# Half of the second MLP product as seven half-size products, with the sums folded into the residual

## The chip, the core and the metric

The kernel runs on one NeuronCore of one Trainium2 chip. The metric is the device time of one execution in microseconds. Three runs of the kernel before gave 973.18, 973.82 and 974.45 us; the median is 973.82 us.

Engine names are those of the profile: PE multiplies matrices (PEld loads its stationary operand), DVE does elementwise work on two tensors, ACT does elementwise work on one tensor and converts types, POOL and SP here mostly issue DMA transfers. Each engine executes its own list of instructions.

## The reference, cut to what matters

One layer of a decoder trunk on 512 tokens of width 1024, in float32. Only the MLP block is touched:

```python
D_MODEL = 1024; SEQ = 512; D_FF = 4 * D_MODEL
h2 = rmsnorm(x, ln2)
x = x + jnp.square(jax.nn.relu(h2 @ w_mlp1)) @ w_mlp2        # (512 x 1024) @ (1024 x 4096), then (512 x 4096) @ (4096 x 1024)
h3 = rmsnorm(x, ln3)
x = x + jax.nn.sigmoid(h3 @ w_pg) * (p @ w_pp)
return rmsnorm(x, ln_f)
```

## The kernel before, in words

**Layout.** Activations lie feature-major: a tile `u` holds 128 features in the partitions and the 512 tokens in the free dimension. The residual is `xx[0..7]`, eight such tiles. The hidden layer of the MLP is `hid[0..31]`, 32 tiles. All `u` tiles come from one pool of `NU` = 71 buffers.

**Precision.** Every product is made in three: each operand is split into a high and a low part of the format that PE reads, and `three` issues high x high, high x low, low x high into one accumulator. A split is one ACT instruction for the high part (`split_hi`, L347 or L349; L236 for weights) and one DVE instruction for the low part (`split_lo`, L355 or L357; L231 for weights).

**Weights.** The host cuts the weights into units of 128 x 1024 numbers (`weight_units`, `_layout`). `OPERANDS` is the order in which PE uses them. When the program asks for operand i with `weight`, `fetch` first emits, for later operands: the low part of operand i+2 (DVE), the high part of i+3 (ACT), sums of weights for i+4, and the load of i+5 (SP). So weights are prepared two operands ahead, in the order of the program. There are four buffers for low parts, five for high parts, six for raw units.

**A plain product** over two 128-feature tiles of input (one "tm" unit, `m2s{sub}.{kk}`) is 24 matmuls with 512 moving columns: 2 input tiles x 4 output tiles x 3. The second MLP product has two halves of its output (`sub` 0 and 1, four PSUM accumulators each) and 16 such units each: 2 x 16 x 24 = 768 matmuls of 512 columns.

**Seven products for eight.** `strassen` multiplies a 2 x 2 block matrix by seven products of half-size blocks instead of eight. Stage i of the seven multiplies one weight operand (A11, S1, A22, S2, A12, S4, S3) by one activation operand (B11, T1, T4, T2, B21, B22, T3) with 24 matmuls of 256 moving columns. S and T are sums or differences of blocks. The S of the weights are made by two DVE additions (L210, L216) and two DMA transfers that add as they write (L202, L213, issued by POOL). The seven products go to four PSUM banks a, c, d, b, with bank a used in stages 0, 3 and 6, c in 1 and 5, d in 2, b in 4. `BEGIN` and `END` say when a bank is read: after stages 0, 1, 2 and 3 the bank is copied to a `u` tile on ACT (`begin`, L322); after stages 4, 5, 6 and 6 the bank is added to such a tile on DVE (`end`, which calls `finish` and `add`, L340). A later stage that writes into the same bank has to wait for the read before it. The first MLP product is eight such groups of seven (`quad`).

**PSUM.** There are two pools of four banks: `mmt` and `smt`. `strassen` takes `mmt`. In the second MLP product `sub` 0 takes its four accumulators from `mmt`, `sub` 1 from `smt`.

**The order around the change** is written by the program itself. `run` issues matmuls in pieces of eight; after each piece `step` takes one item off the list `later`, and, if enough columns have passed (`pace`, 2048 as a rule, which eight matmuls of 256 columns are), advances the generator at the head of the list `side` by one `yield`. So a stage of seven-product work has three steps, and one unit of plain work has three. `drain` steps until both lists are empty without issuing matmuls. The items' instructions go to the engines in the order in which they are emitted.

**After an output half** is complete, four times: `t = psum * norm2` (L1244), `xx += t` (L1245), then `normed` puts on `later` a first item (L349 on ACT: high part; L380 on ACT: square) and, from that, a second item (L357 on DVE: low part; L1111 on DVE: sum of squares).

Of the kernel before, what the change touches and what calls it, by code (L numbers as in the profile page):

```python
# [13 lines left out]
AF = mybir.ActivationFunctionType  # L14
OP = mybir.AluOpType
# [25 lines left out]

def weight_units():
# [13 lines left out]
    def quad(name, src, col, kind="quad"):  # L56
        for m, k in ((0, 0), (1, 0), (1, 1), (0, 1)):
            u.append((f"{name}.A{m + 1}{k + 1}", kind, src, k, col + m * (P if kind == "quad" else 256)))
# [25 lines left out]
    for sub in range(2):  # L84
        for kk in range(16):
            u.append((f"m2s{sub}.{kk}", "tm", "w_mlp2", kk * 2 * P, sub * 512))
# [55 lines left out]
def block_kernel(ctx, tc, xT, ws, pT, wts, wha, wa2, vec, lnf, rel, onehot, ident_d, mask_d, out):  # L142
# [150 lines left out]
    def strassen(name, xo, finish, tm=False, scale=1.0, extra=None):  # L293
# [3 lines left out]
        bank, sums = {}, {}  # L297
# [21 lines left out]
        def begin(c, b):  # L319
            def go():  # L320
                sums[c] = u32()
                S.activation(sums[c], bank[b], AF.Copy, scale=-scale if c[0] else scale)  # L322
            later.insert(0, go)
# [852 lines left out]
    hid = [None] * 32  # L1176
# [4 lines left out]
    def quad(q):  # L1181


        def finish(m, t, s, ps):
            add(m, s, s, ps)

            def positive():
                V.tensor_scalar(s, s, 0.0, None, op0=OP.max)  # L1188

            def act():  # L1190
                for n in range(2):
                    j = 4 * q + 2 * n + m
                    if hid[j] is None:
                        hid[j] = u32()
                    S.activation(hid[j][:, halves(t)], s[:, halves(n)], AF.Square)  # L1195

            later.extend([positive, act])

        def extra(i):
            if i in (3, 4):  # L1200
                later.append(lambda: hid_split(i - 3))

        strassen(f"m1q{q}", x1_op, finish, extra=extra if q == 7 else None)

    hs = {}

    def hid_split(k):
        if k < 32:
            hs[k] = split(hid[k])

    for q in range(8):
        quad(q)
    for k in (2, 3):
        hid_split(k)
# [3 lines left out]
    for sub in range(2):  # L1218
        pss = [mmt() if sub == 0 else smt() for _ in range(4)]
        for kk in range(16):  # L1220
            wh, wl = weight(f"m2s{sub}.{kk}")
            mms = []
            for k in (2 * kk, 2 * kk + 1):
                xh, xl = hs.pop(k)
                for o in range(4):
                    c = slice((k % 2) * 512 + o * P, (k % 2) * 512 + (o + 1) * P)
                    mms += [(pss[o], wh[:, c], xh, k == 0, False), (pss[o], wh[:, c], xl, False, False),
                            (pss[o], wl[:, c], xh, False, k == 31)]
            run(mms)
            for k in (2 * kk + 4, 2 * kk + 5):  # L1230
                hid_split(k if k < 32 or sub else k - 32)
            if sub == 1 and kk == 8:
                for k in range(2):
                    t = u32()
                    GP.dma_start(t, pT[k * P:(k + 1) * P, :])
                    pt.append(split(t))
                for g in range(2):
                    t = u32()
                    GP.dma_start(t, lnf[:, g * 512:(g + 1) * 512].to_broadcast([P, 512]))
                    lnb.append(t)  # L1240
        for o in range(4):
            j = 4 * sub + o
            t = u32()
            V.tensor_tensor(t, pss[o], norm2[1], op=OP.mult)  # L1244
            V.tensor_tensor(xx[j], xx[j], t, op=OP.add)  # L1245
            normed(j, C_LN3, x2s, acc2)
# [126 lines left out]
def _layout(inputs):  # L1373
# [3 lines left out]
    for i, (_, kind, s, r, c) in enumerate(UNITS):  # L1377
# [8 lines left out]
        elif kind == "quad":  # L1386

            a = w.reshape(4, 2, P, -1)[:, r, :, c:c + 3 * P]
# [44 lines left out]
```

## Time and profile before

| what | number |
|---|---|
| median of three runs | 973.82 us |
| the profiled execution, its own time | 974.23 us |
| its span from first to last instruction | 972.4 us |
| granted PE clock, mean | 0.998 |
| first MLP product ends, second begins (on PE) | 730.72 us |
| `sub` 0 ends, `sub` 1 begins | 817.95 us |
| `sub` 1 ends | 904.99 us |

Times inside the span count from its first instruction. In a row of a timeline the columns are: start, length (of the whole group, if it says x2 or more), engine, line, operation, what it writes and reads, and in brackets how long the engine stood idle before it and what it then waited for. The length of an instruction is longer than its distance to the next one on the same engine where the two overlap; both are read below.

### The profile page before, as it was taken

How to read it: one execution, taken by the hardware profiler on the slowest of the kernel's cores; microseconds unless marked ns; L12 is line 12 of the kernel's file. 1: busy time of each engine (PE TensorE's matmuls, PEld its weight loads, DVE VectorE, ACT ScalarE, POOL GpSimd, SP SyncE). 2: the span in 40 equal slices, each digit the busy share in tenths (PEclk: the TensorE clock that was granted, in tenths of full speed). 3: DMA queues.
4: the chain of work that ended last, by engine and by line, in shares of the span. 5: the costliest groups of instructions: out<-in, count | busy, mean ns of one | idle time of the engine just before them, and what ended most of it. 6: DMA issues, size and time to landing. Idle time of an engine off the chain costs nothing.

```text
span 972.4 us, 16047 instructions
## 1 busy us (share of the span) xinstructions
PE 963.5 (99%) x6444; PEld 885.8 (91%) x6444; DVE 694.8 (71%) x988; ACT 524.9 (54%) x878; POOL 96.6 (10%) x137
## 2 busy tenths in 40 slices
PE   9999999999999999999999999999999999999997
PEld 7789999999998999999988889999998888888886
DVE  7788879676788769977855798777676446653654
ACT  7347546345657667575822456556565335442633
POOL 0140010420001021022010000101000000000000
PEclk9999999999999999999999999999999999999999
DMA  8465554974446555546645437566543332533102
GB/s 296 161 197 126 148 139 123 242 205 119 110 120 185 151 131 131 131 131 195 170 112 193 111 64 197 135 169 158 168 132 129 98 98 69 169 91 104 44 1 86
DMA packets 40314, 134.67 MB, mean 138 GB/s; under 512 B 5235, under 2 KB 6847, under 8 KB 40240
## 3 DMA queue, kind: packets, MB, share of 16 engines
q1 hardware_dynamic: 27936, 93.29, 29.1%
q0 software_dynamic: 11008, 38.01, 19.5%
q10 hardware_dynamic: 1296, 2.36, 0.6%
q8 instruction: 50, 0.82, 0.3%
q14 instruction: 24, 0.20, 0.1%
HBM read 127.31 MB, written 8.17 MB: 139 GB/s over the span
## 4 chain that ended last, share of the span: by engine, by line
PE 96%; DVE 2%; issue 1%; DMA 1%; ACT 0%; SPq 0%; POOLq 0%; POOL 0%; DVEq 0%
PE mmt L250 78%; PE smt L250 10%; PE smt L853 1%; PE smt L793 1%; PE smt L719 1%; PE mmt L468 1%; DMA u<-in_xT_dram 1%; PE mmt L469 0%; DVE lo L231 0%; PE mmt L467 0%; DVE ur L355 0%; PE smt L810 0%; PE smt L690 0%; PE smt L809 0%; PE smt L799 0%
## 5 line engine op out<-in xcount | busy, mean ns | idle before, releaser
L250 PE MATMUL mmt<-ur,hi 128*128 128x256 f32 (+1 forms) x2832 | 605.7, 310 | 0.0
L250 PEld LDWEIGHTS mmt<-ur,hi 128*128 128x128 f32 x2832 | 460.4, 188 | 30.0 <-issue 1.9
L250 PE MATMUL mmt<-ur,lo 128*128 128x256 f32 (+1 forms) x1416 | 438.5, 310 | 0.8 <-DVE lo L231 0.8
L231 DVE TENSOR_TENSOR lo<-w,hi 128x1024 fp32r<-128x1024 f32 x239 | 290.1, 1220 | 108.5 <-PE mmt L250 63.6
L236 ACT ACTIVATE hi<-w 128x1024 fp32r<-128x1024 f32 x239 | 250.0, 1054 | 130.1 <-issue 73.1
L250 PEld LDWEIGHTS mmt<-ur,lo 128*128 128x128 f32 x1416 | 266.7, 188 | 15.6 <-DVE lo L231 1.2
L250 PE MATMUL mmt<-hi,ur 128*128 128x256 f32 (+3 forms) x736 | 155.5, 306 | 0.0
L347 ACT ACTIVATE ur<-u 128x512 fp32r<-128x512 f32 x136 | 80.1, 621 | 86.5 <-DVE u L1088 30.9
L250 PEld LDWEIGHTS mmt<-hi,ur 128*128 128x128 f32 x736 | 118.9, 189 | 5.5
L250 PE MATMUL mmt<-lo,ur 128*128 128x256 f32 (+3 forms) x368 | 112.3, 305 | 0.0
L355 DVE TENSOR_TENSOR ur<-u,ur 128x512 fp32r<-128x512 f32 x135 | 88.9, 687 | 17.0 <-ACT ur L347 16.4
L322 ACT ACTIVATE u<-mmt 128x512 f32<-128x512 f32 x96 | 57.0, 593 | 54.2 <-PE mmt L250 54.1
L340 DVE TENSOR_TENSOR u<-u,mmt 128x512 f32<-128x512 f32 (+1 forms) x100 | 62.2, 650 | 32.2 <-PE mmt L250 32.1
L250 PE MATMUL smt<-ur,hi 128*128 128x512 f32 x272 | 83.8, 389 | 0.0
L250 PEld LDWEIGHTS mmt<-lo,ur 128*128 128x128 f32 x368 | 69.4, 189 | 2.6
L250 PEld LDWEIGHTS smt<-ur,hi 128*128 128x128 f32 x272 | 51.1, 188 | 10.7
L250 PE MATMUL smt<-ur,lo 128*128 128x512 f32 x136 | 53.0, 390 | 0.0
L213 POOL DMA_DIRECT2D w<-in_wts_dram x24 | 21.4, 893 | 278.3 <-DVE w L210 166.3
L202 POOL DMA_DIRECT2D w<-in_wts_dram x24 | 21.6, 901 | 237.8 <-DVE lo L231 50.2
L1195 ACT ACTIVATE u<-u 128x256 f32<-128x256 f32 x64 | 23.0, 409 | 30.5 <-DVE u L1188 30.5
L250 PEld LDWEIGHTS smt<-ur,lo 128*128 128x128 f32 x136 | 25.5, 188 | 5.2
L216 DVE TENSOR_TENSOR w<-w 128x1024 f32<-128x1024 f32 x24 | 29.4, 1225 | 0.8
(206 smaller groups left out, 706.4 us busy)
## 6 DMA issues: line engine op xcount, KB each, us to landing
w<-in_wts_dram SPq DMA_DIRECT2D x167, 512.0 KB, 3.9
w<-in_wts_dram POOLq DMA_DIRECT2D x48, 512.0 KB, 5.6
u<-in_xT_dram SPq DMA_DIRECT2D x8, 256.0 KB, 4.9
v_dram<-u POOLq DMA_DIRECT2D x8, 256.0 KB, 7.1
u<-v_dram POOLq DMA_DIRECT2D x8, 256.0 KB, 7.0
y_dram<-u ACTq DMA_DIRECT2D x8, 256.0 KB, 2.3
u<-y_dram POOLq DMA_DIRECT2D x8, 256.0 KB, 7.0
u<-in_xT_dram POOLq DMA_DIRECT2D x8, 256.0 KB, 8.6
```

Source lines behind the costliest of these rows:

```text
L202: GP.dma_start(w, wts[UNIT[f"{q}.A22"]], accum_op=OP.add)
L213: GP.dma_start(w, wts[UNIT[f"{q}.A21"]], accum_op=OP.add)
L216: V.tensor_tensor(w, w, raw[f"{q}.A12"], op=OP.add)
L231: V.tensor_tensor(lo, w, hi.bitcast(F32), op=OP.subtract)
L236: S.activation(hi, w, AF.Copy)
L250: TE.matmul(o, lhsT=l, rhs=r, start=a, stop=b, skip_group_check=shared)
L322: S.activation(sums[c], bank[b], AF.Copy, scale=-scale if c[0] else scale)
L340: V.tensor_tensor(out, s, ps, op=OP.subtract if m else OP.add)
L347: S.activation(hi, x, AF.Copy)
L355: V.tensor_tensor(lo, x, hi.bitcast(F32), op=OP.subtract)
L468: TE.matmul(q0ps[i], lhsT=hi[:, c], rhs=xl, start=False, stop=False)
L1195: S.activation(hid[j][:, halves(t)], s[:, halves(n)], AF.Square)
```

## The change

The 32 hidden tiles are cut into four chunks of eight. Chunks 0 and 2 are multiplied as before ("plain"), chunks 1 and 3 by `strassen` ("seven"), each for both output halves. The order on PE, from the list `MLP2`, is: plain 0 for `sub` 0; seven 1 for `sub` 0; seven 1 for `sub` 1; plain 2 for `sub` 0; seven 3 for `sub` 0; seven 3 for `sub` 1; plain 0 for `sub` 1; plain 2 for `sub` 1. The accumulators of `sub` 0 now come from `smt`, those of `sub` 1 from `mmt`.

`hid_sums` makes the seven activation operands of a chunk, as side work, once for both output halves. The tiles of chunks 1 and 3 are squared in place and kept as blocks (`hb`). The four result tiles of a seven-product group are kept in `msum[sub]`; the second group of the same half is given them as `acc`, and then `begin` is an addition on DVE instead of a copy on ACT. When the last group of a half is done there is a `drain`, and `folds(sub)` is put on `side`: four times a multiplication by `norm2` and two additions of 256 columns into `xx`, and for `sub` 0 after these the four finals (L1244, L1245 and `normed` of before). For `sub` 1 the finals come after the last plain chunk, as before.

The plain chunks 0 and 2 are split once for each output half, as all chunks were. Four splits are put on `later` in the last four stages of the group in front of a plain chunk (`first_splits`). The two small loads for the next product (`pT`, `lnf`) are emitted after the first plain chunk of `sub` 1.

```diff
--- before.py
+++ after.py
@@ -39,6 +39,11 @@
 QUADS = ("quad", "quadt")
 
 
+MLP2 = (("plain", 0, 0), ("seven", 0, 1), ("seven", 1, 1), ("plain", 0, 2), ("seven", 0, 3), ("seven", 1, 3),
+        ("plain", 1, 0), ("plain", 1, 2))
+SEVEN = sorted({c for what, _, c in MLP2 if what == "seven"})
+
+
 def weight_units():
 
     u = []
@@ -53,9 +58,9 @@
 
     fm("q0", "w_in", att_col(0, 0), 4)
     u = u[NS:]
-    def quad(name, src, col, kind="quad"):
+    def quad(name, src, col, kind="quad", chunk=0):
         for m, k in ((0, 0), (1, 0), (1, 1), (0, 1)):
-            u.append((f"{name}.A{m + 1}{k + 1}", kind, src, k, col + m * (P if kind == "quad" else 256)))
+            u.append((f"{name}.A{m + 1}{k + 1}", kind, src, 2 * chunk + k, col + m * (P if kind == "quad" else 256)))
 
     fm("k0", "w_in", att_col(0, 1), 4)
     fm("q1", "w_in", att_col(1, 0), 4)
@@ -81,9 +86,12 @@
     fm("wo", "w_out", 0, 8)
     for q in range(8):
         quad(f"m1q{q}", "w_mlp1", q * 512)
-    for sub in range(2):
-        for kk in range(16):
-            u.append((f"m2s{sub}.{kk}", "tm", "w_mlp2", kk * 2 * P, sub * 512))
+    for what, sub, c in MLP2:
+        if what == "plain":
+            for kk in range(4 * c, 4 * c + 4):
+                u.append((f"m2s{sub}.{kk}", "tm", "w_mlp2", kk * 2 * P, sub * 512))
+        else:
+            quad(f"m2s{sub}c{c}", "w_mlp2", sub * 512, chunk=c)
     for j in range(2):
         u.append((f"pp{j}.0", "tm", "w_pp", 0, j * 512))
     for j in range(2):
@@ -290,11 +298,11 @@
     def halves(t):
         return slice(t * HT, (t + 1) * HT)
 
-    def strassen(name, xo, finish, tm=False, scale=1.0, extra=None):
-
-
-
-        bank, sums = {}, {}
+    def strassen(name, xo, finish, tm=False, scale=1.0, extra=None, acc=None):
+
+
+
+        bank, sums = {}, acc or {}
 
         def stage(op, xname, b):
             wh, wl = weight(f"{name}.{op}")
@@ -318,6 +326,8 @@
 
         def begin(c, b):
             def go():
+                if acc:
+                    return add(c[0], sums[c], sums[c], bank[b])
                 sums[c] = u32()
                 S.activation(sums[c], bank[b], AF.Copy, scale=-scale if c[0] else scale)
             later.insert(0, go)
@@ -1173,7 +1183,7 @@
     side.append(rms_gen(acc1, norm2, 30, 4, True))
 
 
-    hid = [None] * 32
+    hid, hb, hx = [None] * 32, {}, {}
 
     def x1_op(name, pr):
         return cols(xop[name, pr // 2], halves(pr % 2))
@@ -1188,6 +1198,10 @@
                 V.tensor_scalar(s, s, 0.0, None, op0=OP.max)
 
             def act():
+                if q // 2 in SEVEN:
+                    S.activation(s, s, AF.Square)
+                    hb[q, m, t] = s
+                    return
                 for n in range(2):
                     j = 4 * q + 2 * n + m
                     if hid[j] is None:
@@ -1196,54 +1210,147 @@
 
             later.extend([positive, act])
 
+        strassen(f"m1q{q}", x1_op, finish, extra=first_splits(0) if q == 7 else None)
+
+    hs = {}
+    plain = [8 * c + k for what, _, c in MLP2 if what == "plain" for k in range(8)]
+    ahead = [0]
+
+    def hid_splits(n):
+        for k in plain[ahead[0]:ahead[0] + n]:
+            hs[k] = split(hid[k])
+        ahead[0] += n
+
+    def first_splits(n):
+
         def extra(i):
-            if i in (3, 4):
-                later.append(lambda: hid_split(i - 3))
-
-        strassen(f"m1q{q}", x1_op, finish, extra=extra if q == 7 else None)
-
-    hs = {}
-
-    def hid_split(k):
-        if k < 32:
-            hs[k] = split(hid[k])
+            if 3 <= i:
+                later.append(lambda: hid_splits(1))
+        return extra
+
+    def hid_sums(c):
+
+        def blocks(k, t):
+            return [hb[2 * c + g, k, t] for g in range(2)]
+
+        def sums(f, *args):
+            res = [u32() for _ in range(2)]
+            for o, *x in zip(res, *args):
+                f(o, *x)
+            return res
+
+        def less(o, a, b):
+            V.tensor_tensor(o, a, b, op=OP.subtract)
+
+        def splits(name, ts):
+            his = [split_hi(t) for t in ts]
+            yield
+            for g in range(2):
+                hx[name, c, g] = split_lo(ts[g], his[g])
+            yield
+
+        b11, b12, b21, b22 = blocks(0, 0), blocks(0, 1), blocks(1, 0), blocks(1, 1)
+        yield from splits("B11", b11)
+        t1 = sums(less, b11, b12)
+        yield from splits("T1", t1)
+        t2 = sums(minus, t1, b22)
+        yield
+        t4 = sums(minus, t2, b21)
+        yield from splits("T4", t4)
+        yield from splits("T2", t2)
+        yield from splits("B21", b21)
+        yield from splits("B22", b22)
+        t3 = sums(less, b22, b12)
+        yield from splits("T3", t3)
 
     for q in range(8):
         quad(q)
-    for k in (2, 3):
-        hid_split(k)
     drain()
     x2s, acc2 = [None] * KC, []
     pt, lnb = [], []
-    for sub in range(2):
-        pss = [mmt() if sub == 0 else smt() for _ in range(4)]
-        for kk in range(16):
+    pss, msum = [None, None], [{}, {}]
+
+    def fold(sub, m, t):
+
+        x = msum[sub][m, t]
+        x3 = x.rearrange("p (n c) -> p n c", n=2)
+        V.tensor_tensor(x3, x3, norm2[1][:, None, halves(t)].to_broadcast([P, 2, HT]), op=OP.mult)
+        yield
+        for n in range(2):
+            o = xx[4 * sub + 2 * n + m][:, halves(t)]
+            V.tensor_tensor(o, o, x[:, halves(n)], op=OP.add)
+        yield
+
+    def finals(sub):
+
+        for o in range(4):
+            j = 4 * sub + o
+            t = u32()
+            V.tensor_tensor(t, pss[sub][o], norm2[1], op=OP.mult)
+            V.tensor_tensor(xx[j], xx[j], t, op=OP.add)
+            normed(j, C_LN3, x2s, acc2)
+            yield
+
+    def folds(sub):
+        for k in sorted(msum[sub]):
+            yield from fold(sub, *k)
+        yield from finals(sub) if not sub else ()
+
+    def m2_seven(sub, c, last):
+        def finish(m, t, x, ps):
+            add(m, x, x, ps)
+            msum[sub][m, t] = x
+
+        def xo(name, pr):
+            return cols(hx[name, c, pr // 2], halves(pr % 2))
+
+        strassen(f"m2s{sub}c{c}", xo, finish, extra=first_splits(0) if last else None,
+                 acc=msum[sub])
+
+    def m2_plain(sub, c, first, last):
+        if first:
+            pss[sub] = [mmt() if sub else smt() for _ in range(4)]
+        for kk in range(4 * c, 4 * c + 4):
             wh, wl = weight(f"m2s{sub}.{kk}")
             mms = []
             for k in (2 * kk, 2 * kk + 1):
                 xh, xl = hs.pop(k)
                 for o in range(4):
-                    c = slice((k % 2) * 512 + o * P, (k % 2) * 512 + (o + 1) * P)
-                    mms += [(pss[o], wh[:, c], xh, k == 0, False), (pss[o], wh[:, c], xl, False, False),
-                            (pss[o], wl[:, c], xh, False, k == 31)]
+                    w = slice((k % 2) * 512 + o * P, (k % 2) * 512 + (o + 1) * P)
+                    p, a, b = pss[sub][o], first and k == 8 * c, last and k == 8 * c + 7
+                    mms += [(p, wh[:, w], xh, a, False), (p, wh[:, w], xl, False, False), (p, wl[:, w], xh, False, b)]
             run(mms)
-            for k in (2 * kk + 4, 2 * kk + 5):
-                hid_split(k if k < 32 or sub else k - 32)
-            if sub == 1 and kk == 8:
-                for k in range(2):
-                    t = u32()
-                    GP.dma_start(t, pT[k * P:(k + 1) * P, :])
-                    pt.append(split(t))
-                for g in range(2):
-                    t = u32()
-                    GP.dma_start(t, lnf[:, g * 512:(g + 1) * 512].to_broadcast([P, 512]))
-                    lnb.append(t)
-        for o in range(4):
-            j = 4 * sub + o
-            t = u32()
-            V.tensor_tensor(t, pss[o], norm2[1], op=OP.mult)
-            V.tensor_tensor(xx[j], xx[j], t, op=OP.add)
-            normed(j, C_LN3, x2s, acc2)
+
+            if ahead[0] < len(plain) and (kk % 4 < 2 or step_[0] + 1 < len(MLP2) and MLP2[step_[0] + 1][0] == "plain"):
+                hid_splits(2)
+
+    side.append(hid_sums(1))
+    step_ = [0]
+    order = {sub: [i for i, (what, o, _) in enumerate(MLP2) if what == "plain" and o == sub] for sub in range(2)}
+    for i, (what, sub, c) in enumerate(MLP2):
+        step_[0] = i
+        if what == "seven":
+            if sub and c != SEVEN[-1]:
+                side.append(hid_sums(SEVEN[-1]))
+                pace[0] = 6144
+            m2_seven(sub, c, MLP2[i + 1][0] == "plain")
+            pace[0] = 2048
+            if c == SEVEN[-1]:
+                drain()
+                side.append(folds(sub))
+            continue
+        m2_plain(sub, c, i == order[sub][0], i == order[sub][-1])
+        if i == len(MLP2) - 2:
+            for k in range(2):
+                t = u32()
+                GP.dma_start(t, pT[k * P:(k + 1) * P, :])
+                pt.append(split(t))
+            for g in range(2):
+                t = u32()
+                GP.dma_start(t, lnf[:, g * 512:(g + 1) * 512].to_broadcast([P, 512]))
+                lnb.append(t)
+    for _ in finals(1):
+        pass
     while later:
         step()
 
@@ -1385,7 +1492,7 @@
             a = w.reshape(4, 2, P, -1)[:, r, :, c:c + 256].transpose(1, 0, 2)
         elif kind == "quad":
 
-            a = w.reshape(4, 2, P, -1)[:, r, :, c:c + 3 * P]
+            a = w[r // 2 * D:(r // 2 + 1) * D].reshape(4, 2, P, -1)[:, r % 2, :, c:c + 3 * P]
             a = np.stack([a[..., :P], a[..., 2 * P:]], axis=2).transpose(1, 0, 2, 3)
         else:
             a = w[:, c:c + 256].reshape(4, P, 2, P).transpose(1, 2, 0, 3)
```

## The prediction

> **What bounds the kernel now.** I read the page's busy times first, then the chain of work that ended last, then the stages by window. All three in this order:
>
> ```profile
> span 972.4 us, 16047 instructions
> PE 963.5 (99%) x6444; PEld 885.8 (91%) x6444; DVE 694.8 (71%) x988; ACT 524.9 (54%) x878; POOL 96.6 (10%) x137
> ...
> 610.31 207.64 PE mmt L250 x1400
> 817.95 87.04 PE smt L250 x384
> ...
> 581.27:730.72 149.45, 149.45 (x1256) 149.36 (x1257) 113.28 (x135) 91.39 (x149) 10.45 (x12) 1.00 0.61 162
> 730.72:817.95 87.23, 87.23 (x387) 72.24 (x386) 43.80 (x55) 36.26 (x54) 0.00 (x0) 1.00 0.31 98
> 817.95:904.99 87.04, 87.04 (x385) 72.07 (x385) 47.74 (x62) 36.20 (x54) 2.18 (x4) 1.00 0.35 109
> ```
>
> PE is busy 99%; from 610.31 to 904.99 us the chain is nothing but matmuls, at granted clock 1.00. The window rows give PE, PEld, DVE, ACT, POOL: in the seven-product stage (first row) DVE is at 113.28 of 149.45, 76%; in the two plain halves at 43.80 and 47.74 of 87, half idle. So whatever shortens PE's work shortens the kernel, as long as DVE's added work stays out of PE's way. Both have to be priced.
>
> **PE's gain.** The distance between equal events gives the price of a group without its modelled ends. DVE's rows of one seven-product group and of the plain units:
>
> ```profile
> 685.34 0.69 DVE L340 TENSOR_TENSOR u<-u,mmt 128x512 f32<-128x512 f32 x1 [1.57 <-PE mmt L250]
> 686.06 0.43 DVE L1188 TENSOR_SCALAR u<-u 128x512 f32<-128x512 f32 x1
> 686.41 1.22 DVE L231 TENSOR_TENSOR lo<-w,hi 128x1024 fp32r<-128x1024 f32 x1
> 687.66 1.23 DVE L210 TENSOR_TENSOR w<-w 128x1024 f32<-128x1024 f32 x1
> 688.80 0.68 DVE L340 TENSOR_TENSOR u<-u,mmt 128x512 f32<-128x512 f32 x1
> ...
> 691.04 1.29 DVE L340 TENSOR_TENSOR u<-u,mmt 128x512 f32<-128x512 f32 x2
> 692.24 0.42 DVE L1188 TENSOR_SCALAR u<-u 128x512 f32<-128x512 f32 x1
> ...
> 705.28 0.69 DVE L340 TENSOR_TENSOR u<-u,mmt 128x512 f32<-128x512 f32 x1 [1.56 <-PE mmt L250]
> ...
> 747.26 1.23 DVE L231 TENSOR_TENSOR lo<-w,hi 128x1024 fp32r<-128x1024 f32 x1 [2.71 <-PE mmt L250]
> 748.70 1.29 DVE L355 TENSOR_TENSOR ur<-u,ur 128x512 fp32r<-128x512 f32 x2 [0.21 <-ACT ur L347]
> ...
> 807.10 1.23 DVE L231 TENSOR_TENSOR lo<-w,hi 128x1024 fp32r<-128x1024 f32 x1 [2.71 <-PE mmt L250]
> ```
>
> 685.34 and 705.28 are the same addition of two neighbouring groups: 19.94 us for 168 matmuls of 256 columns, 0.1187 us each, 2.85 us a stage. 747.26 and 807.10 are eleven plain units apart: 59.84 / 11 = 5.44 us for 24 matmuls of 512 columns, 0.2267 us each. A chunk of four units costs 21.76 us plain and 19.94 us by seven, 1.82 us less; four times, **7.28 us less**. The arithmetic falls by an eighth, the time by 8.4%, because a short matmul costs more than half a long one.
>
> [...]
>
> **DVE's prices**, as distance to the next instruction, since neighbours overlap:
>
> ```profile
> 580.00 4.62 DVE L231 TENSOR_TENSOR lo<-w,hi 128x1024 fp32r<-128x1024 f32 x4
> ...
> 338.71 0.76 DVE L1045 TENSOR_TENSOR u<-u 128x256 f32<-128x256 f32 x2 [0.70 <-ACT u L1041]
> ...
> 815.94 0.69 DVE L1244 TENSOR_TENSOR u<-mmt,rstd 128x512 f32<-128x512 f32 x1 [6.11 <-PE mmt L250]
> 816.67 0.69 DVE L1245 TENSOR_TENSOR u<-u 128x512 f32<-128x512 f32 x1
> 817.28 0.68 DVE L1244 TENSOR_TENSOR u<-mmt,rstd 128x512 f32<-128x512 f32 x1
> ...
> 908.30 0.74 DVE L357 SCALAR_TENSOR_TENSOR ur<-u,cv,ur 128x512 fp32r<-128x512 f32 x1
> 908.96 0.68 DVE L1111 TENSOR_TENSOR u<-u 128x512 f32<-128x512 f32 x1
> 909.56 0.75 DVE L357 SCALAR_TENSOR_TENSOR ur<-u,cv,ur 128x512 fp32r<-128x512 f32 x1
> ```
>
> Low part of a weight: (4.62 - 1.22) / 3 = 1.13. Weight sum behind it: 688.80 - 687.66 = 1.14, and 0.11 for waiting on that low part (687.66 - 686.41 = 1.25). Any independent 512-column operation (L340 x2, L355 x2): 0.60. 256 columns: 0.76 - 0.42 = 0.34. Fold, not in the trace: its multiplication and dependent addition are priced like L1244 and L1245, 0.73, then two of 0.34: 1.41. Bounds for it: 0.60 + 0.68 below, 0.73 + 0.84 (lengths) above. A final: 0.73 + 0.61 = 1.34. The second item of `normed`: 0.66 + 0.60 = 1.26.
>
> **Where the cover holds.** I added up what each part of the new order puts on DVE, in the order of the lists: plain 0 / `sub` 0: 19.6 of 21.76 us (four low parts, a sum, four splits, sixteen operations of `hid_sums`, the tail of the first product); seven 1 / `sub` 0: 15.2 of 19.94; seven 1 / `sub` 1: 20.5 of 19.94 (low parts 7.9, sum 1.25, four ends 2.4, half of the second `hid_sums` 7.2, three splits 1.8); plain 2: 16 of 21.76; seven 3 / `sub` 0: 14 (low parts 7.9, sums 2.5, four `begin` on DVE 2.4, two ends 1.2). The one overrun, 0.6 us, lies inside the two-operand lead (5.7 us) and is paid back in the plain part behind it; so these cost nothing. Uncovered, it would cost 0.6. The eight extra weight transfers and the eight adding ones are hidden behind the same lead as in the first product, where DMA is at 0.61 and PE never waits:
>
> ```profile
> w<-in_wts_dram SPq DMA_DIRECT2D x167, 512.0 KB, 3.9
> w<-in_wts_dram POOLq DMA_DIRECT2D x48, 512.0 KB, 5.6
> ```
>
> A load is emitted five stages ahead, 14.2 us against 3.9 and 5.6; uncovered, a late one costs up to 5.6 us. Splits go from 64 to 60, ACT loses eight copies; neither is on the path. The small loads (`pT`) come later on POOL, which is otherwise idle there.
>
> **Where it does not hold: seven 3 / `sub` 1.** Behind the `drain`, `folds(0)` yields eight times and the finals of `sub` 0 four times, one per step, so all of it falls into the first four of the seven stages, and the eight `normed` items and four splits for the plain part behind it into the rest. Let T = 0 be PE's start of this group; DVE first does the two ends of the group before, which wait for PE, until 1.3. Then, in emission order (times are DVE's):
> - stage 0: low part, fold, half a fold: 3.9 + 0.7 = 4.6
> - stage 1: low part, sum, `begin`, half a fold, fold: 9.7
> - stage 2: low part (for stage 4, done 10.8, needed 11.4), `begin`, fold, final: 14.2
> - stage 3: low part for stage 5, done 15.3, **needed at 14.25**; `begin`, three finals: 19.9
> - stage 4: low part for stage 6, 21.0; `begin` of bank a, 21.6; stage 6 writes bank a and was **due at 18.2**
> - stages 4 to 6: a second item 0.66, 1.26 twice, two low parts for the plain part, an end, two splits: 28.9
> - `drain`: second item, end of bank c, split, the two ends of bank a: 32.5
>
> As a sum: 1.3 + seven low parts 7.9 + sum 1.25 + four `begin` 2.4 + four folds 5.6 + four finals 5.4 + seconds 0.66 + 3 x 1.26 + three splits 1.8 + four ends 2.4 = **32.5 us of DVE work against 19.94 us of PE work**. The first two bold places hold PE by 1.1 and 3.4 us. The third is the worst: the plain part now takes its four accumulators from `mmt`, four banks, all used by the group before; the last is free when DVE has read bank a, at 32.5. Before, the same hand-over cost nothing, because DVE stood idle and read at once:
>
> ```profile
> 729.13 1.28 DVE L355 TENSOR_TENSOR ur<-u,ur 128x512 fp32r<-128x512 f32 x2
> 730.92 1.28 DVE L340 TENSOR_TENSOR u<-u,mmt 128x512 f32<-128x512 f32 x2 [0.51 <-PE mmt L250]
> ...
> 731.88 0.39 PE L250 MATMUL mmt<-ur,lo 128*128 128x512 f32 x1
> 732.10 0.61 PE L250 MATMUL mmt<-ur,hi 128*128 128x512 f32 x2
> ```
>
> There the ends were read from 730.92 on, PE's plain matmuls ran on without a gap, and the first output tiles needed no late bank. The fourth output tile is the tenth matmul, due at 19.94 + 9 x 0.2267 = 21.98; it starts at 32.5. **PE loses 10.5 us** in all three places together (they are one queue, not to be added twice). Behind it, plain 0 / `sub` 1 has 15.5 us of DVE work in 21.76, so PE is not held again, but PE has no idle time in which to win the loss back.
>
> **Sum:** 974.23 - 7.28 + 10.5 = 977.45 us; the median before is 0.41 us under the profiled execution, so I predict 977.0.
>
> [...] With full lengths in place of distances the 32.5 would be 35.4 and the time 980 us; the rows L340 x2 (1.29 for two of 0.69) show neighbours overlapping, so I stay with distances.
>
> **The rivals.**
> 1. *Absorbed, faster.* The 12.6 us surplus fits into the idle half of the plain parts, as the totals over the whole second product would allow (about 140 us of DVE in 167): 974.23 - 7.28 = 966.95, or 966.5 at the median. It decides if less than 29.3 us of DVE work (32.5 less 10.5 - 7.28) stands ahead of the last read of bank a: for this the second items and splits, 6.2 us, would have to stand behind the ends. Against: the list is first in, first out, and DVE's rows stand in emission order. Chance 0.11.
> 2. *The banks do not hold PE*, only the low parts, bank a and the first splits do: PE's first plain unit then waits for its input's split (done at 25.3, the end of the first split in the list), 25.4 instead of 19.94, and 0.8 more for the second: 6.3 lost, 973.3 in the profile's terms, 972.8, no change. For it: the first accumulators can take banks d and b, free early. Against: there are four banks and four accumulators. Chance 0.12.
> 3. *More waits than I counted.* With up to 66 of 71 `u` buffers alive in seven 1 / `sub` 1 (16 hidden tiles, 8 blocks, 8 of `xx`, 28 operands, 4 results, 2 new high parts), a tile may have to wait for PE to finish a stage; one or two stages more, 2.85 to 5.7: 980 to 983. For: the margin is five buffers. Against: the first product already ran so full without a wait. Chance 0.13.
>
> **How the numbers follow.** The forecast has 0.64; its own range, with the folds at their bounds (-0.5, +0.6) and 3% on DVE's sum (1.0), is 975.5 to 978.6. The range to hold eight in ten reaches down to rival 2 and over most of rival 3: 972 to 982. About 0.2%, 1.95 us, is what a measurement of this kernel can tell from no change. Slower: 0.62 + 0.12 = 0.74 (a little of the forecast's lower edge is given up, and of rival 3); same: rival 2 with those edges, 0.15; faster: rival 1, 0.11.
>
> **What would show it.** PE without waits up to seven 3 / `sub` 1, groups of seven 19.94 us apart; there DVE without idle time for some 32 us, PE waiting three times, for a DVE low part, for the `begin` addition, and for the additions that free `mmt`, some 10 us in all; PE's total near 956. I am wrong if this group takes PE under 22 us to the next plain unit (rival 1), if its wait ends with a split and not with an addition (rival 2), or if PE waits in earlier groups (rival 3).

## The result, and the profile after

The changed kernel takes 980.01 us (median of six runs, 978.3 to 981.91) against 973.8 us: ratio 1.0061, 95% interval 1.0051 to 1.0072. It is slower by 6.2 us. The prediction was 977.0 us, range 972 to 982: the direction and the place are right, the size of the loss came out at nearly twice the forecast 3.2 us. The profiled execution took 981.91 us, the longest of the six and 7.7 us more than the profiled one before: 1.1 us of this lies ahead of the second MLP product (0.8 of it a wait of PE for a load, L718, which the profile before does not have), 6.4 us in it and 0.2 us behind it.

The page of the kernel after:

```profile
span 980.1 us, 16745 instructions
PE 962.9 (98%) x6732; PEld 897.2 (92%) x6732; DVE 748.5 (76%) x1068; ACT 537.5 (55%) x878; POOL 103.6 (11%) x145
```

PE has 288 matmuls more (four groups of 168 for four of 96) and is busy 0.6 us less: not the 7.3 us that the forecast took off, since waits that are short, matmuls at a lower clock and the slower pace of the new groups (all below) count as busy. The windows of the kernel after, one row for each part of the second MLP product (times, then PE, PEld, DVE, ACT, POOL, then granted clock, DMA share, GB/s); the second-last row runs from the start of seven 3 / `sub` 1 to the tenth matmul behind it, the last from there to the end of the product (912.62 lies 0.14 us inside the next one):

```profile
731.83:754.06 22.23, 22.11 (x98) 17.95 (x97) 18.34 (x28) 13.83 (x23) 0.00 (x0) 1.00 0.34 76
754.06:774.30 20.24, 20.24 (x170) 20.24 (x169) 19.01 (x21) 12.16 (x16) 2.65 (x3) 1.00 0.49 133
774.30:794.55 20.25, 20.25 (x170) 20.25 (x169) 18.11 (x24) 13.39 (x19) 0.88 (x1) 1.00 0.69 180
794.55:816.36 21.81, 21.81 (x99) 18.03 (x98) 18.85 (x26) 11.06 (x18) 0.87 (x1) 1.00 0.44 106
816.36:836.60 20.24, 20.24 (x171) 20.24 (x170) 13.44 (x15) 7.34 (x8) 0.87 (x1) 1.00 0.46 125
836.60:869.02 32.42, 25.31 (x178) 23.16 (x176) 32.14 (x49) 16.61 (x24) 2.18 (x4) 0.90 0.51 144
869.02:912.62 43.60, 43.60 (x184) 35.92 (x185) 25.79 (x38) 12.11 (x17) 0.00 (x0) 0.95 0.33 97
```

In the row from 836.60 DVE is busy 32.14 of 32.42 us. Its rows there are the list of the prediction, one by one; the first, the middle and the last:

```profile
836.56 1.28 DVE L350 TENSOR_TENSOR u<-u,mmt 128x512 f32<-128x512 f32 x2 [2.08 <-PE mmt L258]
837.76 1.22 DVE L239 TENSOR_TENSOR lo<-w,hi 128x1024 fp32r<-128x1024 f32 x1
838.90 0.69 DVE L1277 TENSOR_TENSOR u<-u,rstd 128x512 f32<-128x512 f32 x1
839.62 0.76 DVE L1281 TENSOR_TENSOR u<-u 128x256 f32<-128x256 f32 x2
...
857.27 0.68 DVE L350 TENSOR_TENSOR u<-u,mmt 128x512 f32<-128x512 f32 x1
...
867.60 1.27 DVE L350 TENSOR_TENSOR u<-u,mmt 128x512 f32<-128x512 f32 x2
```

L350 is the addition that was L340: the two ends of the group before, the `begin` of bank a, the two ends of bank a. L1277 and L1281 are the fold. With T = 0 at 836.5 the `begin` ends at T + 21.4 (forecast 21.6) and the last end at T + 32.4 (forecast 32.5). PE's waits in the same stretch (idle before, and what ended it):

```profile
851.69 0.39 PE L258 MATMUL mmt<-ur,lo 128*128 128x256 f32 x1 [0.53 <-DVE lo L239]
...
858.09 0.47 PE L258 MATMUL mmt<-ur,hi 128*128 128x256 f32 x2 [3.53 <-DVE u L350]
...
864.76 0.70 PE L258 MATMUL mmt<-ur,hi 128*128 128x512 f32 x2 [1.37 <-DVE u L350]
...
867.13 1.22 PE L258 MATMUL mmt<-ur,hi 128*128 128x512 f32 x2 [1.44 <-DVE u L350]
868.15 0.63 PE L258 MATMUL mmt<-ur,lo 128*128 128x512 f32 x1
869.02 1.19 PE L258 MATMUL mmt<-ur,hi 128*128 128x512 f32 x2 [0.24 <-DVE u L350]
870.01 0.63 PE L258 MATMUL mmt<-ur,lo 128*128 128x512 f32 x1
```

A low part, the `begin` of bank a, then three times the ends that free a bank, as forecast. New is the distance of the last rows: 0.99 us from 869.02 to 870.01 for two matmuls that take 0.46 elsewhere. The windows of this stretch say why (the clock is the third number from the end):

```profile
859.35:862.75 3.40, 3.40 (x17) 3.33 (x16) 3.40 (x6) 3.40 (x6) 0.67 (x2) 0.50 0.78 228
862.75:866.15 3.40, 1.57 (x6) 0.67 (x4) 3.40 (x6) 3.25 (x6) 0.94 (x2) 1.00 0.93 294
866.15:872.95 6.80, 5.58 (x12) 3.97 (x13) 6.76 (x12) 0.00 (x0) 0.00 (x0) 0.50 0.35 106
872.95:912.48 39.53, 39.53 (x176) 32.67 (x175) 21.75 (x32) 11.97 (x17) 0.00 (x0) 1.00 0.34 99
```

The granted clock falls to half twice. The first time is behind the gap of 3.53 us, from 859.35 to 862.75 us; PE then waits for DVE again (to 864.76), so this stretch costs nothing of its own. Then the clock is full again, and it falls a second time among the waits for the banks: from 862.75 to 866.15 PE is busy for 1.57 of 3.40 us, with no single wait over 1.44 us. This second stretch lasts until 872.95 us and reaches 3.9 us beyond the last wait.

### The profile page after: what moved, and what is told of

It is laid out like the page before. It is cut to its first block, busy times and chain, and to the rows that moved or that the text cites. A ratio compares the mean times of both kernels' runs of the same rounds, so it can differ in the third digit from the quotient of the medians.

```text
span 980.1 us, 16745 instructions
## 1 busy us (share of the span) xinstructions
PE 962.9 (98%) x6732; PEld 897.2 (92%) x6732; DVE 748.5 (76%) x1068; ACT 537.5 (55%) x878; POOL 103.6 (11%) x145
## 3 DMA queue, kind: packets, MB, share of 16 engines
q0 software_dynamic: 12160, 42.20, 21.6%
## 4 chain that ended last, share of the span: by engine, by line
PE 91%; DVE 6%; issue 1%; DMA 1%; ACT 1%; SPq 0%; POOLq 0%; POOL 0%; DVEq 0%; ACTq 0%
PE mmt L258 78%; PE smt L258 4%; PE smt L863 1%; DVE lo L239 1%; DVE ur L365 1%; PE smt L803 1%; PE smt L729 1%; DVE u L350 1%; DMA u<-in_xT_dram 1%; PE mmt L478 1%; PE mmt L479 0%; DMA u<-s_dram 0%; PE mmt L477 0%; PE smt L820 0%; PE smt L700 0%
## 5 line engine op out<-in xcount | busy, mean ns | idle before, releaser
L258 PE MATMUL mmt<-ur,hi 128*128 128x256 f32 (+1 forms) x3152 | 650.9, 304 | 6.6 <-DVE u L350 6.6
L258 PEld LDWEIGHTS mmt<-ur,hi 128*128 128x128 f32 x3152 | 508.5, 189 | 33.5 <-issue 4.6
L258 PE MATMUL mmt<-ur,lo 128*128 128x256 f32 (+1 forms) x1576 | 479.6, 304 | 1.4 <-DVE lo L239 1.4
L258 PEld LDWEIGHTS mmt<-ur,lo 128*128 128x128 f32 x1576 | 298.7, 190 | 14.2 <-DVE lo L239 2.0
L350 DVE TENSOR_TENSOR u<-u,mmt 128x512 f32<-128x512 f32 (+1 forms) x124 | 78.3, 657 | 40.7 <-PE mmt L258 40.7
L332 ACT ACTIVATE u<-mmt 128x512 f32<-128x512 f32 x104 | 61.6, 592 | 61.8 <-PE mmt L258 61.8
L258 PE MATMUL smt<-ur,hi 128*128 128x512 f32 x144 | 44.7, 391 | 0.1
L218 DVE TENSOR_TENSOR w<-w 128x1024 f32<-128x1024 f32 x28 | 34.3, 1225 | 1.0
L224 DVE TENSOR_TENSOR w<-w 128x1024 f32<-128x1024 f32 x28 | 34.3, 1225 | 1.0
L258 PEld LDWEIGHTS smt<-ur,hi 128*128 128x128 f32 x144 | 26.9, 188 | 6.0 <-DVE ur L365 0.5
L258 PE MATMUL smt<-ur,lo 128*128 128x512 f32 x72 | 28.2, 392 | 0.0
L390 ACT ACTIVATE u<-u 128x512 f32<-128x512 f32 x24 | 14.9, 621 | 17.6 <-DVE u L1179 17.6
```

The source lines that it names most:

```text
L218: V.tensor_tensor(w, w, raw[f"{q}.A11"], op=OP.add)
L224: V.tensor_tensor(w, w, raw[f"{q}.A12"], op=OP.add)
L258: TE.matmul(o, lhsT=l, rhs=r, start=a, stop=b, skip_group_check=shared)
L350: V.tensor_tensor(out, s, ps, op=OP.subtract if m else OP.add)
L390: S.activation(t, x, AF.Square, scale=1.0 / 32.0)
```

## The experiments

All times are medians, beside runs of the kernel before on the same chip. Theory throughout: DVE's list in seven 3 / `sub` 1 holds PE, the half clock follows from the gap.

### The folds moved behind the group

```diff
             if c == SEVEN[-1]:
                 drain()
-                side.append(folds(sub))
+                if sub:
+                    side.extend([folds(0), folds(1)])
```

> The folds and finals of sub 0 no longer stand in the group seven 3 / sub 1: both folds(0) and folds(1) are side work of the two plain chunks behind it. Theory (DVE's queue in that group holds PE): DVE has 17.6 us of work there instead of 33, under 19.94 us, so PE is not held; the 10.5 us of waiting and the 1.9 us of matmuls at half clock behind it go, and the time is about 967.6 us, ratio 0.994 to before. Rival (the loss lies in the seven-product groups themselves, their traffic and their buffers): PE still waits about as long and the time stays at 978 to 980 us.

Measured: 968.01 us against 973.58, ratio 0.9943 (0.993 to 0.9955). PE has no wait in the whole second product after the first chunk. Chain rows of this kernel:

```profile
752.58 40.33 PE mmt L258 x336
792.91 21.81 PE smt L258 x96
814.72 85.25 PE mmt L258 x534
```

The same work in another place makes a loss of 6.2 us a gain of 5.6. That is the theory's number within 0.4 us; the loss was in the place of the folds, not in the groups.

### The accumulators in other banks

```diff
-            pss[sub] = [mmt() if sub else smt() for _ in range(4)]
+            pss[sub] = [smt() for _ in range(4)]
```

> As the changed kernel, but the accumulators of sub 1 come from the other four banks, smt, which are free once the finals of sub 0 have read them (855.5 us in the trace of the changed kernel). DVE's order and work are the same. Theory: the first plain unit no longer waits for the two ends of bank a; its tenth matmul comes at about 864.4 (full clock) to 866.2 us (half clock) instead of 869.0, and less of the time lost to the half clock lies on the path: 974.5 to 977 us. The waits for the low part and for the begin of bank a, 4 us, remain. Rival (the banks do not matter, PE waits for the splits): the wait moves to the split of the first hidden tiles and the time stays within 1 us of 980.

Measured: 974.27 us against 973.58, ratio 1.0007 (0.9998 to 1.0016). DVE does the same list, and two of PE's waits are left, the low part and the `begin`; the plain part starts at 860.60 us without one. The last row is the chain's, 192 plain matmuls in one piece:

```profile
849.75 0.39 PE L258 MATMUL mmt<-ur,lo 128*128 128x256 f32 x1 [0.53 <-DVE lo L239]
856.15 0.61 PE L258 MATMUL mmt<-ur,hi 128*128 128x256 f32 x2 [3.53 <-DVE u L350]
...
860.76 43.53 PE smt L258 x192
```

The hand-over of the four banks was worth 5.7 us at the medians. Between the two profiles it is 6.4 us: 4.4 is the wait itself (the tenth plain matmul at 28.0 us behind the group's start instead of 32.4), 2.0 the second stretch of half clock, which does not come. The first one is still there, behind the same gap:

```profile
856.34:859.74 3.40, 3.40 (x17) 3.40 (x17) 3.40 (x6) 3.40 (x7) 0.55 (x1) 0.50 0.74 193
```

It now lies on PE's path: the last stage takes 4.45 us (856.15 to 860.60) instead of 2.85. The time was 0.2 us better than the lower edge I gave, for I had left part of the half clock behind the wait. The rival, a wait for the first split, did not show: that split ran on DVE at 858.99, and PE, slowed by the half clock, came to the plain part at 860.60.

### The reads of the banks ahead of the rest

```diff
         def end(c, b):
-            later.append(lambda: finish(*c, sums[c], bank[b]))
+            if acc:
+                later.insert(0, lambda: finish(*c, sums[c], bank[b]))
+            else:
+                later.append(lambda: finish(*c, sums[c], bank[b]))
```

> As the changed kernel, but in the second group of each half the reads of the banks after stages 4, 5 and 6 go to the head of the list instead of its end. No work is taken away. In seven 3 / sub 1 a second item (1.26 us) and two splits (1.2 us) then stand behind the last read of bank a. Theory: that read ends 2.45 us earlier, PE's tenth plain matmul with it, and the time is 977.5 us, or up to 1 us less where the half clock is shorter too. Rival (PE waits for the total of DVE's work or for the splits, not for the place in the queue): no change, 980 us.

Measured: 975.96 us against 973.58, ratio 1.0025 (1.0015 to 1.0035).

```profile
834.78 1.29 DVE L353 TENSOR_TENSOR u<-u,mmt 128x512 f32<-128x512 f32 x2 [2.08 <-PE mmt L258]
...
863.35 1.27 DVE L353 TENSOR_TENSOR u<-u,mmt 128x512 f32<-128x512 f32 x2
```

and PE's waits at the head of the plain part:

```profile
862.22 0.50 PE L258 MATMUL mmt<-ur,hi 128*128 128x512 f32 x1 [1.06 <-DVE ur L368]
...
864.77 0.70 PE L258 MATMUL mmt<-ur,hi 128*128 128x512 f32 x2 [0.41 <-DVE u L353]
865.30 0.39 PE L258 MATMUL mmt<-ur,lo 128*128 128x512 f32 x1
```

No instruction was removed; 2.46 us of them stand behind the last read instead of in front, and PE starts 30.0 us behind the group's start instead of 32.4. So it is the place in DVE's list that counts. The other 1.6 us of the 4.0 gained (2.0 between the profiles) are the second stretch of half clock: here the clock falls once, behind the gap of 3.53 us that this kernel has too, and is full again when PE reaches the plain part:

```profile
856.48:859.88 3.40, 3.40 (x17) 3.40 (x17) 3.40 (x6) 3.40 (x7) 0.55 (x1) 0.50 0.84 196
859.88:870.00 10.12, 8.65 (x41) 6.78 (x40) 10.09 (x16) 6.12 (x10) 1.06 (x2) 1.00 0.53 172
```

The time is 0.5 us under the range I gave (976.5 to 977.5), which had at most 1 us for the half clock. Now a split (L368) holds PE for 1.06 us, as rival 2 of the prediction had it for this place.

### Gaps of other sizes in the kernel before

Is it the gap that brings the half clock? Additions of no use on DVE in the plain stage, where nothing of the change is, make PE wait once:

```diff
         for kk in range(16):
+            if sub == 0 and kk == 8:
+                t = u32()
+                for _ in range(32):      # 36 and 26 in the other two
+                    V.tensor_tensor(t, xx[0], xx[1], op=OP.add)
```

> The kernel before with 32 additions of no use on DVE in front of the ninth plain unit of sub 0, so that PE has to wait once, by an estimate from DVE's rows for 1.9 us. Theory (the half clock in the changed kernel came from a PE gap of 3.5 us): a gap of under 3 us leaves the granted clock at 1.00, and the time rises by the gap itself, to about 975.5 us. Rival (any wait of PE is followed by matmuls at half clock): 1.5 to 2 us more than the gap, and rows of the windows behind the gap with a clock near 0.5.

> As the short gap, with 36 additions: PE waits by the same estimate for 4.3 us. Theory: after the gap the granted clock is near 0.5 for 3 to 4 us, in which 512-column matmuls take 0.43 us instead of 0.227, and the time rises by the gap and 1.6 to 2 us more: about 979.7 us. Rival (the slow matmuls came from the seven-product group or from DVE's traffic, not from the gap): the gap alone, 977.9 us, clock 1.00.

Measured: 981.03 and 984.45 us against 973.69, ratios 1.0077 (1.0062 to 1.0092) and 1.011 (1.0095 to 1.0125). My estimates of the gaps were 3.8 and 4.3 us short, so the first of them was no short gap; I think that I had let DVE run further ahead than it does. The waits, and the windows at half clock; first with 32 additions, then with 36:

```profile
790.72 0.79 PE L250 MATMUL mmt<-ur,hi 128*128 128x512 f32 x1 [5.70 <-DVE ur L355]
...
790.36:793.76 3.40, 3.04 (x7) 2.46 (x8) 3.40 (x6) 0.00 (x0) 0.00 (x0) 0.50 0.61 172
```

```profile
793.68 0.79 PE L250 MATMUL mmt<-ur,hi 128*128 128x512 f32 x1 [8.61 <-DVE ur L355]
...
788.40:798.62 10.22, 4.94 (x12) 3.88 (x13) 10.08 (x14) 0.00 (x0) 0.00 (x0) 0.50 0.35 103
```

7.34 us are lost for a gap of 5.70 and 10.76 for one of 8.61: 1.6 and 2.1 us more than the gap, with the clock at half for 3.0 and 4.9 us behind it (from 790.72 to 793.76, and from 793.68 to 798.62). There is no seven-product group near. A third kernel with a gap that is really short:

> The kernel before with 26 additions of no use on DVE at the place where 32 of them made PE wait 5.70 us and 36 made it wait 8.61 us. At 0.61 us an addition the gap is 5.70 - 3.66 = 2.0 us. Theory (the clock falls only behind a gap of about 3.5 us or more, as behind the 3.53 us of the changed kernel, and not behind the 1.06 us of the run with the ends first): matmuls at full pace behind it, clock 1.00, time 973.7 + 2.0 = 975.7 us. Rival (any gap of this size): 977.2 us or more.

Measured: 975.42 us against 973.62, ratio 1.0019 (1.0009 to 1.0028), 1.8 us for a gap whose row says 1.34:

```profile
784.29 0.39 PE L250 MATMUL mmt<-ur,hi 128*128 128x512 f32 x1
786.02 0.50 PE L250 MATMUL mmt<-ur,hi 128*128 128x512 f32 x1 [1.34 <-DVE ur L355]
786.36 0.39 PE L250 MATMUL mmt<-ur,lo 128*128 128x512 f32 x1
786.59 0.62 PE L250 MATMUL mmt<-ur,hi 128*128 128x512 f32 x2
787.06 0.40 PE L250 MATMUL mmt<-ur,lo 128*128 128x512 f32 x1
```

The row counts the idle time from the modelled end of the matmul before; by the starts, 784.29 to 786.02 where 0.23 us is usual, PE loses 1.5 us. Behind it three matmuls take 0.70 us (786.36 to 787.06), within 0.02 us of full pace (3 x 0.2267), although the same kind of additions runs on DVE. So the single gaps of 3.53, 5.70 and 8.61 us were followed by the half clock and the single gap of 1.34 us was not; between 1.34 and 3.53 us nothing was tried. In the changed kernel the second fall, at 866.15 us, came some 0.5 us into the wait of 1.44 us, with the wait of 1.37 us shortly ahead of it; no run varied the work between such waits.

### The first chunk's 0.4 us

```diff
+            if i_ == 0 and kk < 2:        # i_: place in MLP2
+                hid_splits(2)
             run(mms)
-            if ahead[0] < len(plain) and (...):
+            if i_ and ahead[0] < len(plain) and (...):
                 hid_splits(2)
```

on top of the late folds.

> The late folds, and in the first plain chunk the two splits that follow a unit are emitted ahead of its matmuls, so ahead of the side work of hid_sums in the lists of ACT and DVE. Theory (the 0.4 us that PE lost there, 22.2 instead of 21.8 us for that chunk, was a split standing behind hid_sums): that chunk takes 21.8 us and the time is 967.6 us. Rival (PE waited for a weight or a buffer): 968.0 us.

Measured: 967.67 us against 973.69, ratio 0.9937 (0.9922 to 0.9952). The chain now has the chunk in one piece, where the late folds and the changed kernel had it broken by a wait for a split:

```profile
730.70 21.78 PE smt L258 x96
752.48 40.33 PE mmt L258 x336
```

22.23 to 21.78 us: the split stood behind `hid_sums` in the lists. Against the late folds the gain of 0.3 us is not clear of the intervals; the row is.

### The price of a group

The last row also has 40.33 us for two groups, 20.16 each, where the prediction took 19.94. What is different at 19.94? In the first product of the kernel before, the pace of the 256-column matmuls is 0.1200 us from 600 to 610 us and 0.1187 right after, with two matmuls of another kind between (L410, L411); earlier it changes too, at 575 us (behind a wait of 0.5 us) and 600 us. Four kernels put matmuls of no use in front of each of the four groups; the first two on the late folds, the others on the early splits:

```diff
+            if fresh and b == "a" and name.startswith("m2s"):
+                mms.insert(0, mms[0])                      # one more of 256 columns
+                # or twice, or once:
+                TE.matmul(bank[b][:, 0:n], lhsT=ones_r, rhs=..., start=True, stop=True)   # n = 512, 128, 128
             run(mms, shared=True)
```

> The late folds, and in the first stage of each of the four seven-product groups of the second MLP product the first matmul is issued twice (0.12 us each, 0.5 us together). The question is why such a group takes 20.2 us there and 19.94 us in the first product. Theory A (it depends on how the run of 256-column matmuls is entered, and one matmul more shifts it): groups of 19.94 + 0.12 us, time 967.5 us. Theory B (it lies in the operands or in what runs beside): groups of 20.3 us, time 968.5 us.

Measured: 968.22 us against 973.69, ratio 0.995 (0.9933 to 0.9967). Two groups take 40.56 us, 0.23 more for the two added matmuls: no change of pace, as theory B had it.

> The late folds, and in front of each of the four seven-product groups of the second MLP product two matmuls of 512 columns of no use, whose result the first matmul of the group wipes out. In the first MLP product the pace of the 256-column matmuls went from 0.1200 to 0.1187 us at the place where two such matmuls stand (610 us, L410 and L411). Theory: the pace is set by how the run is entered, groups of 19.94 + 0.45 us, 968.0 + 0.6 us. Rival: it is not, groups of 20.2 + 0.45 us, 969.8 us.

Measured: 968.88 us against 973.62, ratio 0.9949 (0.993 to 0.9969). The theory holds here, against what the run before suggested: the groups run at 19.93 us behind 0.47 us for the two:

```profile
752.82 0.47 PE mmt L327 x2
753.28 19.93 PE mmt L258 x168
```

> Late folds and early splits together, and in front of each of the four seven-product groups of the second MLP product two matmuls of 128 columns of no use. With two of 512 columns the groups took 19.93 us instead of 20.2, at a cost of 0.47 us each. Theory (what counts is that matmuls of another kind stand between, not how wide they are): groups of 19.94 us behind about 0.12 us, 967.67 - 4 x (0.27 - 0.12) = 967.1 us. Rival (the width counts): groups of 20.2 us, 968.1 us.

Measured: 968.13 us against 973.91, ratio 0.9939 (0.9925 to 0.9952); neither theory. A group behind a plain chunk keeps the slow pace, a group behind a group gets the fast one:

```profile
752.76 0.17 PE mmt L327 x2
752.93 20.21 PE mmt L258 x168
773.14 0.17 PE mmt L327 x2
773.32 19.99 PE mmt L258 x168
```

> As the two narrow matmuls, with only one. Theory (an even or odd number decides, as one matmul of 256 columns did not change the pace): groups of 20.2 us, 967.9 us. Rival (any foreign matmul at the entry does it): groups of 19.94 us, 966.8 us.

Measured: 966.99 us against 973.91, ratio 0.9929 (0.9915 to 0.9942). The theory of even and odd numbers is out. One narrow matmul, 0.06 us, and all groups run near the fast pace:

```profile
752.56 0.06 PE mmt L327
752.62 19.99 PE mmt L258 x168
```

So there are two paces, and what stands ahead of the run decides between them: one of 128 columns or two of 512 give the fast one, one more of 256 columns or (behind a plain chunk) two of 128 the slow one. Width, number and time of the entry all differ among these, and which of them counts is open. With late folds and early splits this is the fastest version found, 6.9 us under the kernel before.

## Why the prediction was right, and where it was not

The forecast for the stretch from the first to the last matmul of the second product was 174.27 - 7.28 + 10.5 = 177.5 us; the trace has 180.7 (731.83 to 912.48, where the next product starts). By its own steps:

| step | forecast, us | trace after, us |
|---|---|---|
| plain 0 / `sub` 0 | 21.76 | 22.23 |
| seven 1, both halves | 39.88 | 40.49 |
| plain 2 / `sub` 0 | 21.76 | 21.81 |
| seven 3 / `sub` 0 | 19.94 | 20.24 |
| start of seven 3 / `sub` 1 to the tenth matmul behind it | 32.5 | 32.42 |
| from there to the end | 41.48 | 43.46 |

Of the 3.3 us by which the trace is over the sum of the forecasts, 0.5 is plain 0 / `sub` 0, 0.9 the pace of the groups and 2.0 the last row.

**DVE's queue.** Right in place, order and size. The list of emitted instructions with the distances from the trace before gave every one of DVE's times to 0.4 us, and the tenth matmul to 0.1. So the 980 us that the prediction worked out with full lengths, 35.4 us for the list, is the measured time only by chance: the list took 32.4. The folds, which the trace before did not have, were priced by L1244 and L1045 at 1.41 and measured 0.72 + 0.68. The three kernels that move work out of the way, or the banks, or only the order, gained 12.0, 5.7 and 4.0 us; the first came out 0.4 us above its number, the other two 0.2 and 0.5 us below their ranges, which had priced the half clock too low.

**The step that failed is "PE loses 10.5 us in all three places together", with nothing behind it.** The 10.5 us themselves are right: 32.42 - 21.98 = 10.4. But PE's clock falls to half among the waits (0.50 from 866.15 to 872.95 us), and nine to ten matmuls behind the last of them take 0.43 us instead of 0.227: 2.0 us, the whole difference in the last row of the table. What costs this is the second stretch of half clock, among and behind the waits for the banks. The gap of 3.53 us alone does not do this: the kernels with other banks and with the reads ahead have the same gap, and their matmuls behind the tenth run at full pace. The kernel before had no gap over 0.5 us in that stage, so its trace could not show it; the gaps of 5.70 and 8.61 us put into the kernel before did. Of the single gaps, those of 3.53, 5.70 and 8.61 us had the half clock behind them and the one of 1.34 us had not; the second stretch began with no wait over 1.44 us since the clock was full again. The prediction gave 3.4 us for the wait in the middle (3.53 in the trace) and priced every matmul behind it at the full pace.

**The gain of PE was over-sized:** 1.82 us a group was taken from groups at the fast pace, and the four groups run at the slow one, 20.2 us. That is 0.2 to 0.3 us each, 0.9 us in the table's second and fourth rows, and 6.1 to 6.4 us of gain in place of 7.28. With one narrow matmul in front the price of the prediction returns to 0.05 us.

**"The cover holds" was wrong for one place by 0.4 us:** in plain 0 / `sub` 0 the sum of DVE's work (19.6 in 21.76, 18.3 measured) fits, but a split that is due early stands behind `hid_sums`. A sum over a part does not see an order within it; in the group where I went through the order stage by stage, it was right. Three smaller readings of that part were wrong without a cost. Seven 1 / `sub` 0 has DVE busy for 19.01 us, not 15.2. There are no eight extra weight loads, only the eight adding ones (SPq x167 on both pages, POOLq x48 and x56). And ACT does not lose eight copies against the kernel before but gains eight (L322 x96, L332 x104).

**The rivals.** Rival 1 (all absorbed) is out for this order; with the folds in the two plain chunks behind the group it is what happens, 968.0 instead of 966.5. Rival 2 (the banks do not hold PE) is out: other banks give back 5.7 us. Its number, 972.8, would be the kernel with other banks, which measured 974.3, 1.5 more, the half clock of seven 3 / `sub` 1's last stage. Rival 3 (waits for buffers in seven 1 / `sub` 1) did not show: that window has PE busy throughout.

**The range.** The forecast's own range, 975.5 to 978.6 us, does not hold the 980.0. The wide one, 972 to 982, does, but its upper part was there for rival 3, which did not occur: that it covered the half clock and the slower groups is luck.

## What to carry to other kernels

When an engine with idle time takes over side work, add up its list between two points at which the bounding engine needs something from it, in the order of emission, and not over the stage: here 32.5 us of work stood in a window of 20 while the stage as a whole had room, and moving the same work into the two plain chunks behind it turned 0.6% slower into 0.6% faster. Look at what hands a scarce resource back (the last read of a PSUM bank) and put it first in the list (4.0 us here). A gap of the matrix engine can cost more than its length: those of 5.70 and 8.61 us cost 7.34 and 10.76 here, and behind the waits of 1.37, 1.44 and 0.24 us for the banks 2.0 us went to the half clock; price such gaps with it, as far as no other wait covers it.

## What the runs showed of the hardware that was not expected

The runs of 256-column matmuls, each with its own load of the stationary operand, kept one of two paces here, 0.1187 or 0.1200 us, through hundreds of matmuls, and a single matmul of 128 columns (0.06 us) in front of a group took it from 20.16 to 19.99 us. The clock fell with a delay: 3.3 to 5.3 us after the start of the gaps of 3.53, 5.70 and 8.61 us, in the changed kernel only 1.3 us after PE had begun to work again. The stretches at half clock behind gaps and waits measured 3.4 us (four times), 6.8 us (the second one of the changed kernel) and 10.2 us (the gap of 8.61 us), so one, two and three times the same length. PE ran at full clock again 3.0 to 4.9 us after a single gap had ended. The six runs of the changed kernel spread over 3.6 us and those of the kernel before over 1.3; no run shows why.
